# Sample-token projection in float32 on column quarters, and merge gates in a PSUM bank of their own

## The chip, the cores and the metric

One core of one Trainium2 chip runs the whole program. The metric is device time in microseconds of one execution: the median over several executions. PE is the matrix engine (TensorE), PEld its weight loads, DVE, ACT and POOL the vector, scalar and GpSimd engines, SP the queue that issues nearly all DMAs.

## The reference

One layer of a mixer is computed for 1024 prompt tokens and 32 sample tokens ("dec" in the code) that share all weights:

```
h   = rms_norm(x, g_norm) * (1 + scale) + shift            # scale, shift, gate = silu(c) @ w_ada
qa, ka, va, ga, qb, kb, vb, gb, mg = split(h @ w_in)       # 6144 columns, mg is 2048 of them
oa  = diff_attn(rms(qa), rms(ka), va)    # 4 heads, two softmax maps each, block-causal
ob  = band_attn(rms(qb), rms(kb), vb)    # 8 heads, own 64-chunk and the 8 before it
m   = sigmoid(mg_a) * ((oa*silu(ga)) @ w_oa) + sigmoid(mg_b) * ((ob*silu(gb)) @ w_ob)
out = x + gate * (m @ w_out)             # also returned: the keys and values of both branches
```

The sample tokens attend to 128 cached rows besides their own 32. Inputs and outputs are float32.

## The kernel before, in words

Float32 products are made on PE from float32r pieces. `get_w(u, k)` loads a 128x512 weight tile `wr` (a ring of 3 buffers for all weights), ACT rounds it to `wh`, DVE makes the rest `wl = wr - wh`, and a product of two split operands is three matmuls: high by high, high by low, low by high. `wh` and `wl` have 8 buffers each for the projection, and 2 each (`mh`, `ml`) for the merge gates and later weights.

The program has four stages.

1. Start: conditioning (`ada`, float32 matmuls of 32 weight columns, four of them side by side on column quarters of PE, tile `pm`), the RMS norm, and the split input `H[k]`. The 32 sample columns of `H[k]`, high and low side by side, are copied by POOL to `HS[k]` (128x64). Four early row tiles of unit 0 are projected here.
2. Units: eight units, u = 0 to 3 of branch A (512 weight columns) and 4 to 7 of branch B (384, and the gates `pg`). In each, row tiles t = 0 to 7 of 128 prompt tokens and t = 8, the sample tokens, are projected (`proj_items`: eight items k in a row into a bank `pp`), normed (`norm`), transposed (`tr`), scored (`s`), exponentiated, transposed again (`pt`, copied to `pr` by ACT and DVE) and multiplied by the values (`o`); branch A also transposes its result (`zt`). Query and key pieces go through DMAs (`split` to `qs` and `kc`). For t = 8 the projection is 16 float32r matmuls with `HS[k]` as weights (high and low, 64 columns) against `wh` and `wl`; DVE copies and adds the two halves (`dsrc`). After t = 8, `get_w` is called for all of the next unit.
   Of the 48 merge-gate thirds (24 matmuls of 352 columns each into `mg`, a Tanh on ACT, a store `tgd`), `MERGE` puts 24 after chosen row tiles of the units. They take the same two banks `pj` as the projections (the first two take `o` and `pt`) and stand in line with them.
3. Merge rest: the other thirds, while `load_z` brings back the attention results and splits them.
4. Output: `y` (the two branch projections), the merge, and `out`, on PE without a pause.

The order of work is made on the host. A small clock simulation first puts items in program order: attention items that are ready go first, the others ("flat") fill in, not more than `LEAD` row tiles ahead. Then `Plan.flush` schedules every instruction with a cost model: on PE the ready instruction that stands first in program order is taken; on the other engines the one with the longest tail. Instructions are emitted in that order, and each engine runs its own in order. PSUM has eight banks: `pj` 2, `tq` 1, `s` 2, `pt` 2, `o` 1.

Of the kernel before, what the change touches and what calls it, by code (L numbers as in the profile page):

```python
# [35 lines left out]
FIRST = ("o", "pt")  # L36

# [3 lines left out]
MERGE = ((5, 5, 8), (7, 8, 8), (7, 8, 8), (7, 8, 8), (8, 8), (7, 7, 8), (7, 7, 8), (7, 8, 8, 8))  # L41


class Buf:


    def __init__(self, shape, space, make, real=None):
        self.shape, self.space, self.make, self.real = list(shape), space, make, real
        self.writes, self.reads, self.ops, self.dtype = [], [], [], F32
        self.before = self.last = None  # L50
# [69 lines left out]
class Tiles:  # L120


    def __init__(self, pool, space="SB", bufs=1):
        self.pool, self.space, self.bufs, self.tags = pool, space, bufs, {}

    def tile(self, shape, dtype, name, tag=None, bufs=None, padded_shape=None):
# [5 lines left out]
        b.dtype = dtype  # L132
# [19 lines left out]
class Engine:  # L152
# [15 lines left out]
    def cost(self, method, outs, ins, kw):  # L168
# [25 lines left out]
class Plan:  # L194
# [10 lines left out]
    def __init__(self, nc):  # L205
# [4 lines left out]
        self.like, self.urge = None, 0.0  # L210
# [9 lines left out]
    def record(self, eng, cost, f, outs, ins, args, kw):  # L220
# [5 lines left out]
        op.like, op.urge = self.like, self.urge  # L226
# [43 lines left out]
    def flush(self, in_turn=False):  # L270

        self.link()
# [11 lines left out]
        pe = [op for op in self.ops if op.eng == "PE"]  # L284
# [29 lines left out]
        while len(order) < len(self.ops):  # L314
# [32 lines left out]
        for op in sorted(order, key=lambda o: o.start):  # L347
            op.emit()
        for op in self.ops:
            op.preds = op.succs = op.emit = op.acc = None  # L350
        self.ops = []
# [3 lines left out]
def hybrid_mixer_step(ctx: ExitStack, tc: tile.TileContext, xT, cT, two, c_rows, w_as, w_ag, b_ada, g_norm, w_all,  # L355
                      g_rows, g_sub, lam, bias_a, bias_b, ck, cv,
                      y, akp, avp, bkp, bvp, aks, avs, bks, bvs):
    nc = tc.nc
    plan = Plan(nc)
# [16 lines left out]
    BANKS = {"pj": 2, "tq": 1, "s": 2, "pt": 2, "o": 1}  # L376
# [19 lines left out]
    wtiles = {}  # L396

    def get_w(u, k):
# [4 lines left out]
        load(wr, w_all[u, k])  # L403
        split_hi_lo(wh, wl, wr, S, V)
        wtiles[u, k] = (wh, wl)

# [9 lines left out]
    HS = [hp.tile([P, 2, NS], F32R, name=f"HS{k}") for k in range(KT)]  # L416


    with tc.tile_pool(name="start", bufs=1) as spool:
# [106 lines left out]
        def modulate(i, k):  # L526
# [8 lines left out]
            if i:  # L535
                G.tensor_copy(HS[k], H[k][:, :, NP:NT].bitcast(F32))

# [50 lines left out]
    class Item:  # L588
        def __init__(self, emit, dur, lat, bank=None, hold=0.0):
            self.emit, self.dur, self.lat, self.bank, self.hold = emit, dur, lat, bank, hold  # L590

        def ready(self, prev):
            r = prev + self.lat * LATENCY
# [4 lines left out]
        def run(self, prev):  # L598
            clk.now = max(clk.now, self.ready(prev)) + self.dur
            if self.bank:  # L600
                clk.bank_used(self.bank[0], clk.now + self.hold * LATENCY)
            self.emit()
            return clk.now
# [4 lines left out]
    with ExitStack() as uctx:  # L608
# [43 lines left out]
        def proj_items(un, t, st):  # L652
# [4 lines left out]
            def mm(k):  # L657
# [4 lines left out]
                if not dec:  # L662
                    for i, (a, b) in enumerate(((0, wh), (0, wl), (1, wh))):
                        PE.matmul(pp[:, :wcols], lhsT=H[k][:, a, t * P:(t + 1) * P], rhs=b[:, :wcols],
                                  start=(k == 0 and i == 0), stop=(k == 7 and i == 2))
                else:
                    for i, b in enumerate((wh, wl)):
                        PE.matmul(pp[:64, :wcols], lhsT=HS[k].rearrange("p a b -> p (a b)"), rhs=b[:, :wcols],
                                  start=(k == 0 and i == 0), stop=(k == 7 and i == 1))
                if k == 7:  # L670
                    norm()

            def norm():
                src = st["pp"]
                if dec:
                    pp, src = src, up.tile([P, 512], F32, tag="split", name=f"dsrc{u}")
                    V.tensor_copy(src[:n, :wcols], pp[32:64, :wcols])
                    V.tensor_tensor(out=src[:n, :wcols], in0=pp[:n, :wcols], in1=src[:n, :wcols], op=ALU.add)
# [43 lines left out]
            if dec:  # L722
                d *= 2 / 3
# [8 lines left out]
        def attn_items(un, t, st):  # L732
# [176 lines left out]
            for m in range(1 if isA else 2):  # L909
# [4 lines left out]
                for g in range(len(groups)):  # L914
# [4 lines left out]
                                      bk("o") if last else None, 1.0))  # L919
# [4 lines left out]
        def mg_items(i, c, ci, tag):  # L924

            u, d, b = 8 + i, 2 * i + c // 2, c % 2
            o, w = CHN[ci]
            st = {}

            def mm(k):  # L930
                if k == 0:
                    st["p"] = tile_bank(tag, f"mg{d}_{b}_{ci}")
                pg = st["p"]
                wh, wl = wtiles[u, 2 * c + k // 4]
                for j, (a, hb) in enumerate(((wh, 0), (wh, 1), (wl, 0))):
                    PE.matmul(pg[:, :w], lhsT=a[:, (k % 4) * P:(k % 4 + 1) * P], rhs=H[k][:, hb, o:o + w], start=(k == 0 and j == 0), stop=(k == 7 and j == 2))
                if k == 7:
                    tg = up.tile([P, 352], F32, tag="tg", name=f"tg{d}_{b}_{ci}")
                    S.activation(tg[:, :w], pg[:, :w], AF.Tanh, scale=0.5)
                    store(tgd[d, :, b, o:o + w], tg[:, :w])  # L940

            dd = 3 * (w / 2400 + 0.003)
            return [Item(lambda k=k: mm(k), dd, 0.0, bk(tag) if k == 0 else None, 9 * dd + (1.0 if tag == "pj" else 9.0)) for k in range(KT)]


        flat = []
        steps = []
        clk.free = {}
        proj_end = {}
        for t, tag in enumerate(EARLY):  # L950
            proj_end[t] = 1.2 * t
            clk.bank_used(tag, 4.0 + 1.2 * t)
        mgn = [0]

        def mg_chunk(step):
            r = mgn[0]
            if r == 48:
                return
            mgn[0] += 1
            g, ci = r // 3, r % 3  # L960
            flat.extend((step, it, None) for it in mg_items(g // 4, g % 4, ci, FIRST[r] if r < len(FIRST) else "pj"))
            if ci == 2 and g < 15:
                flat[-1] += ([lambda g=g: fm_w(g + 1)],)

        fm_w(0)
        for u in range(8):
            un = UN[u] = Unit(u)
            for t in range(9):
                st = {}
                steps.append((un, t, st))  # L970
                fl = []
                if not un.isA and t in (0, 3, 6):
                    fl += [(it, None) for it in gate_items(un, t // 3)]
                its = proj_items(un, t, st)
                if u == 0 and t < len(EARLY):
                    st["pp"] = early[t]
                    st["norm"]()
                    continue
                fl += [(it, None) for it in its[:-1]] + [(its[-1], len(steps) - 1)]
                flat += [(len(steps) - 1, it, mark) for it, mark in fl]  # L980
                if t == 8:
                    post = [lambda u=u: [get_w(u + 1, k) if u < 7 else fm_w(16 + k) for k in range(8 if u < 7 else 3)]]
                    flat[-1] += (post,)
                for _ in range(MERGE[u].count(t)):
                    mg_chunk(len(steps) - 1)
            if u == 7:
                n_attn = len(flat)
        while mgn[0] < 48:
            mg_chunk(len(steps))

        fi = 0
        active = []
# [252 lines left out]
```

## Time and profile before

| | us |
|---|---|
| median of 3 runs | 1044.6 (1041.18 to 1045.16) |
| the profiled execution, time | 1041.39 |
| the profiled execution, span in the profile | 1039.6 |
| PE busy | 999.7 (96%) |
| DVE, ACT, POOL busy | 660.3, 453.8, 262.7 |

The span runs from the first to the last instruction. All instructions carry line 223, that of the recording helper, so rows are told apart by tile names: `pp<-wh,HS` is a matmul into `pp` that reads `wh` and `HS`. A matmul's shape is given as weight rows * weight columns, then rows x streamed columns. Matmuls overlap: the time that one takes is read from the start of one to the start of the next, not from its duration. The code of a float32 matmul leaves two matmul records (64 in the code of `ada`, 128 in the trace).

### The profile page before, as it was taken

The page shows a single profiled execution, that of the slowest core. Times are in us where ns is not written, and L with a number is a line of the kernel's source. Part 1 is how long each engine was busy: PE and PEld are TensorE (multiplying, and loading weights), DVE is VectorE, ACT ScalarE, POOL GpSimd, SP SyncE. Part 2 cuts the span into 40 slices and gives each one's busy share as a digit, 9 for nine tenths or more (in the row PEclk, how much of TensorE's full clock was granted, in tenths as well). Part 3 has the DMA queues.
Part 4 walks back from the last instruction along what each step waited for, and adds up shares of the span by engine and source line. Part 5 has one row for each costly group of instructions (what it writes and reads, how often), then busy time and mean ns, then how long its engine had stood idle before and what let it go on. Part 6 is the DMA issues. An engine that isn't in the chain of part 4 may idle for free.

```text
span 1039.6 us, 19092 instructions
## 1 busy us (share of the span) xinstructions
PE 999.7 (96%) x6016; PEld 911.6 (88%) x6016; DVE 660.3 (64%) x1936; ACT 453.8 (44%) x1306; POOL 262.7 (25%) x348
## 2 busy tenths in 40 slices
PE   3998989999999999999999999999999999999998
PEld 2666868887887889898999999899989999999998
DVE  4685785784785677588578678767944117975221
ACT  3463564563564455456355445545635212212000
POOL 0254324423433432322221331222200002331000
PEclk9998999999999999999999999999999999999999
DMA  9623433343324225224323322422456327665421
GB/s 328 257 78 84 144 108 79 82 127 98 84 83 143 78 74 168 57 69 125 91 74 112 116 64 77 145 77 70 118 184 196 99 86 227 212 195 174 145 91 49
DMA packets 136803, 126.55 MB, mean 122 GB/s; under 512 B 24064, under 2 KB 113024, under 8 KB 136576
## 3 DMA queue, kind: packets, MB, share of 16 engines
q1 hardware_dynamic: 135696, 124.98, 40.2%
q8 instruction: 49, 0.80, 0.3%
q14 instruction: 50, 0.41, 0.1%
q10 hardware_dynamic: 1008, 0.35, 0.1%
HBM read 75.46 MB, written 23.86 MB: 96 GB/s over the span
## 4 chain that ended last, share of the span: by engine, by line
PE 82%; DVE 5%; DMA 4%; SPq 3%; issue 2%; ACT 2%; POOL 1%; ACTq 0%; DVEq 0%; POOLq 0%
PE pp L223 27%; PE mg L223 16%; PE out L223 9%; PE y L223 9%; PE s L223 6%; PE o L223 5%; PE pg L223 4%; PE pt L223 3%; SPq L223 3%; DMA qs<-split 2%; PE tr L223 1%; DVE T L223 1%; DMA wr<-in_w_all_dram 1%; PE pm L223 1%; DVE x L223 1%
## 5 line engine op out<-in xcount | busy, mean ns | idle before, releaser
L223 PE MATMUL pp<-wh,H 128*128 128x512 f32 (+1 forms) x1024 | 319.1, 377 | 5.1 <-DVE qn L223 2.7
L223 PEld LDWEIGHTS pp<-wh,H 128*128 128x128 f32 x1024 | 187.2, 190 | 28.4 <-DVE H L223 3.2
L223 PE MATMUL pp<-wl,H 128*128 128x512 f32 (+1 forms) x512 | 192.3, 376 | 0.0
L223 PE MATMUL mg<-H,wh 128*128 128x352 f32 x768 | 189.5, 326 | 0.9 <-ACT wh L223 0.9
L223 PEld LDWEIGHTS mg<-H,wh 128*128 128x128 f32 x768 | 133.1, 188 | 3.2 <-ACT wh L223 1.4
L223 ACT ACTIVATE T<-T,nm 128x640 f32<-128x640 f32 (+5 forms) x144 | 101.0, 701 | 76.9 <-DVE nm L223 74.1
L223 DVE TENSOR_TENSOR wl<-wr,wh 128x512 fp32r<-128x512 f32 x128 | 92.9, 733 | 56.0 <-ACT wh L223 55.9
L223 PE MATMUL mg<-H,wl 128*128 128x352 f32 x384 | 124.2, 325 | 0.0
L223 ACT ACTIVATE wh<-wr 128x512 fp32r<-128x512 f32 x128 | 79.6, 629 | 88.9 <-DMA wr<-in_w_all_dram 40.4
L223 PE MATMUL s<-kc,qs 128*128 128x512 f32 (+3 forms) x384 | 100.0, 341 | 7.8 <-DMA qs<-split 7.4
L223 PEld LDWEIGHTS pp<-wl,H 128*128 128x128 f32 x512 | 97.0, 189 | 11.2 <-issue 2.1
L223 POOL TENSOR_TENSOR v<-vraw,v 128x128 fp32r<-128x128 f32 (+1 forms) x72 | 36.0, 502 | 255.5 <-ACT v L223 245.6
L223 DVE CUSTOM_DVE_ANT_0 T<-s,bias 128x512 f32<-128x512 f32 (+2 forms) x144 | 73.8, 512 | 34.0 <-PE s L223 32.4
L223 PE MATMUL y<-Z,wh 128*128 128x352 f32 x384 | 92.4, 323 | 0.0
L223 PE MATMUL out<-MT,wh 128*128 128x352 f32 (+2 forms) x384 | 92.1, 323 | 0.0
L223 DVE TENSOR_TENSOR pr<-pt,pr 128x512 fp32r<-128x512 f32 (+5 forms) x168 | 76.0, 460 | 18.3 <-ACT pr L223 16.4
L223 POOL TENSOR_TENSOR ssq<-ssq,mhalf 128x4 f32<-128x4 f32 (+1 forms) x72 | 75.9, 1054 | 45.5 <-DVE ssq L223 29.8
L223 ACT ACTIVATE pr<-pt 128x512 fp32r<-128x512 f32 (+5 forms) x168 | 65.5, 412 | 49.7 <-PE pt L223 35.2
L223 PEld LDWEIGHTS s<-kc,qs 128*128 128x128 f32 x384 | 66.9, 190 | 17.4 <-issue 9.9
L223 PEld LDWEIGHTS mg<-H,wl 128*128 128x128 f32 x384 | 72.0, 188 | 0.4
L223 POOL TENSOR_TENSOR tgl<-tgl,tgl 128x352 f32<-128x352 f32 x24 | 28.3, 1180 | 174.2 <-DMA tgl<-tgd 107.1
L223 POOL TENSOR_TENSOR qn<-qn,grow 128x256 f32<-128x256 f32 (+1 forms) x72 | 57.4, 799 | 52.1 <-DVE qn L223 29.7
(131 smaller groups left out, 1770.9 us busy)
## 6 DMA issues: line engine op xcount, KB each, us to landing
wr<-in_w_all_dram SPq DMA_DIRECT2D x128, 256.0 KB, 3.1
kc<-split SPq DMA_DIRECT2D x256, 64.0 KB, 2.1
tgd<-tg SPq DMA_DIRECT2D x48, 176.0 KB, 2.5
tgl<-tgd SPq DMA_DIRECT2D x48, 176.0 KB, 3.3
wa<-in_w_as_dram SPq DMA_DIRECT2D x16, 512.0 KB, 8.1
qs<-split SPq DMA_DIRECT2D x256, 32.0 KB, 1.9
zr<-zd SPq DMA_DIRECT2D x24, 176.0 KB, 3.8
wg<-in_w_ag_dram SPq DMA_DIRECT2D x16, 256.0 KB, 3.3
```

The lines of the kernel that those rows point to most:

```text
L223: f(*[r(x) for x in args], **{k: r(v) for k, v in kw.items()})
```

## The change: what it does

- The sample tokens' projection reads `wr`, the unsplit float32 weights. `HS[k]` becomes the float32 sum of the two pieces (128x32); for each k, four (branch B: three) float32 matmuls of 128 columns, one for each 128 weight columns, go to the four column quarters of PE, into 32 partitions each of one bank. ACT copies the bank to SBUF, and later, when t = 7 is normed, copies the quarters side by side.
- For units 1 to 7 these items stand at the head of the unit, after `get_w` of that unit, and not at its end; `get_w` follows t = 7 of the unit before. For unit 0 the eight tiles are loaded once more and the items alternate with those of t = 5.
- Merge thirds get a bank `mg` of their own; `pt` has one bank in place of two. Their matmuls are marked `low`: they are not in PE's program order, and the planner takes one only when no other PE instruction is ready. `MERGE` puts 26 thirds into the units. A load of merge weights is planned to wait until its `wh` buffer is free.
- The clock simulation runs twice; in the second run an item also waits until the buffers that it took in the first are free (`Item.free`).
- The planner's cost of a 32-column float32 matmul goes from 0.0675 to 0.108 us for 256 columns.

```diff
-FIRST = ("o", "pt")
-MERGE = ((5, 5, 8), (7, 8, 8), (7, 8, 8), (7, 8, 8), (8, 8), (7, 7, 8), (7, 7, 8), (7, 8, 8, 8))
+MERGE = 7 * ((0, 0, 1, 0, 1, 0, 1, 0, 0),) + ((0, 0, 1, 0, 1, 0, 1, 1, 2),)
...
-                return 0.0675 * max(n, 64) / 256 if ins[0].shape[-1] == 32 else max(1.69e-3 * n, 0.22)
+                return 0.4225e-3 * max(n, 64) if ins[0].shape[-1] == 32 else max(1.69e-3 * n, 0.22)
...
-        pe = [op for op in self.ops if op.eng == "PE"]
+        pe = [op for op in self.ops if op.eng == "PE" and not op.low]
...
-                heapq.heappush(avail[e], (op.idx if e == "PE" else -op.tail, i, op))
+                heapq.heappush(avail[e], (op.idx + (1e6 if op.low else 0) if e == "PE" else -op.tail, i, op))
...
-    BANKS = {"pj": 2, "tq": 1, "s": 2, "pt": 2, "o": 1}
+    BANKS = {"pj": 2, "tq": 1, "s": 2, "pt": 1, "o": 1, "mg": 1}
...
         load(wr, w_all[u, k])
+        if mg and plan.units:
+            plan.ops[-1].acc.append((wh.view(), False))
         split_hi_lo(wh, wl, wr, S, V)
         wtiles[u, k] = (wh, wl)
+        if u < 8:
+            wraw[u, k] = wr
...
-                G.tensor_copy(HS[k], H[k][:, :, NP:NT].bitcast(F32))
+                G.tensor_tensor(out=HS[k], in0=H[k][:, 0, NP:NT].bitcast(F32), in1=H[k][:, 1, NP:NT].bitcast(F32), op=ALU.add)
...
-                else:
-                    for i, b in enumerate((wh, wl)):
-                        PE.matmul(pp[:64, :wcols], lhsT=HS[k].rearrange("p a b -> p (a b)"), rhs=b[:, :wcols],
-                                  start=(k == 0 and i == 0), stop=(k == 7 and i == 1))
...
+            def mm_dec(k):
+                if u == 0:
+                    wr = wp.tile([P, 512], F32, tag="wr", name=f"wd{k}", bufs=3)
+                    load(wr, w_all[0, k])
+                else:
+                    wr = wraw[u, k]
+                if k == 0:
+                    st["pp"] = tile_bank("pj", f"pp{u}_{t}")
+                for j in range(wcols // P):
+                    PE.matmul(st["pp"][32 * j:32 * j + 32, :P], lhsT=HS[k], rhs=wr[:, j * P:(j + 1) * P], start=(k == 0), stop=(k == 7))
+                if k == 7:
+                    st["raw"] = up.tile([P, P], F32, tag="dsrc", name=f"dsrc{u}")
+                    S.activation(st["raw"][:wcols // 4], st["pp"][:wcols // 4, :P], AF.Copy)
...
                 if dec:
-                    pp, src = src, up.tile([P, 512], F32, tag="split", name=f"dsrc{u}")
-                    V.tensor_copy(src[:n, :wcols], pp[32:64, :wcols])
-                    V.tensor_tensor(out=src[:n, :wcols], in0=pp[:n, :wcols], in1=src[:n, :wcols], op=ALU.add)
+                    src = up.tile([P, 512], F32, tag="split", name=f"src{u}")
+                    for j in range(wcols // P):
+                        S.activation(src[:n, j * P:(j + 1) * P], st["raw"][32 * j:32 * j + 32], AF.Copy)
...
+        def mg_third(r):
+            g, ci = r // 3, r % 3
+            d, b = g // 2, g % 2
             o, w = CHN[ci]
+            plan.low = True
+            pg = tile_bank("mg", f"mg{d}_{b}_{ci}")
+            for k in range(KT):
+                wh, wl = wtiles[8 + g // 4, 2 * (g % 4) + k // 4]
                 for j, (a, hb) in enumerate(((wh, 0), (wh, 1), (wl, 0))):
                     PE.matmul(pg[:, :w], lhsT=a[:, (k % 4) * P:(k % 4 + 1) * P], rhs=H[k][:, hb, o:o + w], start=(k == 0 and j == 0), stop=(k == 7 and j == 2))
+            tg = up.tile([P, 352], F32, tag="tg", name=f"tg{d}_{b}_{ci}")
+            S.activation(tg[:, :w], pg[:, :w], AF.Tanh, scale=0.5)
+            store(tgd[d, :, b, o:o + w], tg[:, :w])
+            plan.low = False
             if ci == 2 and g < 15:
+                fm_w(g + 1)
...
+                        if t == 7:
+                            fl[-1] = (its[7], now, [dec[u]["norm"]])
+                    flat += [(now, it, mark, post or []) for it, mark, post in fl]
+                    if t == 7:
+                        flat[-1][3].extend(lambda k=k, u=u: get_w(u + 1, k) if u < 7 else fm_w(16 + k) for k in range(8 if u < 7 else 3))
+                    if t == 8 and u < 7:
+                        dec.append({})
+                        flat += [(now, it, None, []) for it in proj_items(UN.setdefault(u + 1, Unit(u + 1)), 8, dec[-1])]
+                    flat[-1][3].extend([merge] * MERGE[u][t])
...
+        back = plan.mark()
+        kept = dict(wtiles), dict(wraw)
+        lay_out()
+        back()
...
-        return tile_bank(("pj", "s", "pt")[banks[0] % 3], name)
+        return tile_bank(("pj", "s", "mg", "pj", "s", "pt")[banks[0] % 6], name)
```

## Rows read from the trace of the kernel before

**Rows 1.** The page: engines, chain of work that ended last, by engine.

```profile
PE 999.7 (96%) x6016; PEld 911.6 (88%) x6016; DVE 660.3 (64%) x1936; ACT 453.8 (44%) x1306; POOL 262.7 (25%) x348
...
PE 82%; DVE 5%; DMA 4%; SPq 3%; issue 2%; ACT 2%; POOL 1%; ACTq 0%; DVEq 0%; POOLq 0%
```

**Rows 2.** Busy by stretch: eight units, merge rest, output (PE, PEld, DVE, ACT, POOL; clock, DMA).

```profile
60.00:108.00 48.00, 41.13 (x184) 32.57 (x183) 32.45 (x104) 23.49 (x78) 25.30 (x37) 0.89 0.35 94
108.00:204.00 96.00, 92.30 (x507) 76.28 (x506) 69.25 (x227) 54.48 (x175) 36.37 (x54) 1.00 0.37 103
204.00:297.00 93.00, 90.44 (x499) 75.68 (x498) 62.45 (x192) 47.74 (x150) 33.38 (x48) 1.00 0.35 98
297.00:381.00 84.00, 83.62 (x455) 69.75 (x454) 56.76 (x184) 43.83 (x142) 33.71 (x48) 1.00 0.36 102
381.00:466.00 85.00, 83.40 (x528) 78.81 (x527) 61.02 (x187) 44.44 (x131) 22.89 (x32) 1.00 0.35 97
466.00:562.00 96.00, 94.73 (x612) 90.03 (x611) 74.98 (x241) 49.95 (x153) 25.55 (x33) 1.00 0.32 88
562.00:649.00 87.00, 86.37 (x553) 82.08 (x552) 66.82 (x214) 44.81 (x136) 22.31 (x29) 1.00 0.36 99
649.00:757.00 108.00, 104.97 (x676) 99.06 (x675) 83.88 (x264) 58.95 (x174) 25.73 (x34) 1.00 0.38 109
757.00:850.00 93.00, 92.43 (x575) 91.87 (x574) 24.52 (x52) 30.48 (x69) 0.00 (x0) 1.00 0.42 133
850.00:1040.00 190.00, 186.39 (x1161) 186.18 (x1159) 95.86 (x198) 30.22 (x55) 28.33 (x24) 1.00 0.50 157
```

**Rows 3.** PE's timeline in unit 0, where it sits idle; start, duration, idle before.

```profile
91.00 0.40 PE L223 MATMUL o<-v,pr 128*128 128x256 f32 x2
93.15 0.59 PE L223 MATMUL s<-kc,qs 128*128 128x384 f32 x2 [1.75 <-DMA qs<-split]
...
98.08 1.19 PE L223 MATMUL s<-kc,qs 128*128 128x512 f32 x2 [0.62 <-DMA qs<-split]
```

**Rows 4.** Busy time by stretch, same columns, where the clock is slow.

```profile
96.47:106.71 10.24, 8.71 (x23) 5.85 (x23) 5.64 (x18) 3.43 (x10) 1.44 (x2) 0.50 0.32 82
```

**Rows 5.** PE's timeline: sample-token matmuls of 512 columns, then of 384.

```profile
109.90 0.39 PE L223 MATMUL pp<-wl,HS 128*64 128x512 f32 x1
110.13 0.40 PE L223 MATMUL pp<-wh,HS 128*64 128x512 f32 x1
...
466.55 0.34 PE L223 MATMUL pp<-wl,HS 128*64 128x384 f32 x1
466.72 0.33 PE L223 MATMUL pp<-wh,HS 128*64 128x384 f32 x1
```

**Rows 6.** PE's timeline: float32 matmuls on column quarters among full ones.

```profile
25.66 1.07 PE L223 MATMUL pm<-wa,c 128*32 128x256 f32 x16
26.66 0.50 PE L223 MATMUL pp<-wh,H 128*128 128x512 f32 x1
...
28.60 0.64 PE L223 MATMUL pm<-wa,c 128*32 128x256 f32 x8
29.17 0.50 PE L223 MATMUL pp<-wh,H 128*128 128x512 f32 x1
29.51 0.39 PE L223 MATMUL pp<-wl,H 128*128 128x512 f32 x1
29.73 0.63 PE L223 MATMUL pp<-wh,H 128*128 128x512 f32 x2
30.29 0.64 PE L223 MATMUL pm<-wa,c 128*32 128x256 f32 x8
```

**Rows 7.** PE's timeline: float32r matmuls of 32 weight columns among full ones.

```profile
231.44 0.31 PE L223 MATMUL s<-kd,qs 128*32 128x160 f32 x2
231.59 0.66 PE L223 MATMUL pp<-wh,H 128*128 128x512 f32 x2
232.09 0.39 PE L223 MATMUL pp<-wl,H 128*128 128x512 f32 x1
```

**Rows 8.** Groups of instructions, shapes apart, 60 to 757 us: busy, mean ns.

```profile
L223 DVE TENSOR_TENSOR wl<-wr,wh 128x512 fp32r<-128x512 f32 x79 | 56.6, 727 | 6.3 <-ACT wh L223 6.1
L223 ACT ACTIVATE wh<-wr 128x512 fp32r<-128x512 f32 x80 | 49.8, 631 | 18.5 <-DMA wr<-in_w_all_dram 16.7 <-PE mg L223 1.0
L223 DVE TENSOR_TENSOR pr<-pt,pr 128x512 fp32r<-128x512 f32 x64 | 43.5, 685 | 8.5 <-ACT pr L223 8.0
L223 ACT ACTIVATE pr<-pt 128x512 fp32r<-128x512 f32 x64 | 37.5, 593 | 27.1 <-PE pt L223 16.1 <-PE o L223 10.6
L223 DVE COPY dsrc<-pp 32x512 f32<-32x512 f32 x4 | 2.7, 682 | 0.1
L223 ACT ACTIVATE vraw<-dsrc 32x128 f32<-32x128 f32 x8 | 2.3, 293 | 0.0
```

**Rows 9.** DMA issues by line: count, KB each, median us to landing.

```profile
wr<-in_w_all_dram SPq DMA_DIRECT2D x128, 256.0 KB, 3.1
qs<-split SPq DMA_DIRECT2D x256, 32.0 KB, 1.9
```

**Rows 10.** Instructions that touch `wr`: duration ns min/median/max, first and last start.

```profile
L223 SPq DMA_DIRECT2D wr<-in_w_all_dram x128: 327/371/1507, 8.3 to 980.4; - x128
```

More of the change, by code (lines that the diff above doesn't have):

```diff
@@ L209, in __init__ @@
         self.rows = {"DVE": None, "ACT": None}
-        self.like, self.urge = None, 0.0
+        self.like, self.urge, self.low, self.units = None, 0.0, False, True
         self.V, self.S, self.G, self.PE = (Engine(self, n, e) for n, e in (
@@ L270, in flush, with mark, back, lay_out @@
     def flush(self, in_turn=False):
+        for op in self.lay_out(in_turn):
+            op.emit()
+        for op in self.ops:
+            op.preds = op.succs = op.emit = op.acc = None
+        self.ops = []
+    def mark(self):
+        bufs = [(b, list(b.writes), list(b.reads), list(b.ops)) for b in Buf.made]
+        rings = [(r, {t: list(q) for t, q in r.tags.items()}) for r in Tiles.made]
+        free, ring, rows = dict(self.free), self.ring, dict(self.rows)
+        def back():
+            del Buf.made[len(bufs):]
+            for b, w, r, o in bufs:
+                b.writes, b.reads, b.ops = list(w), list(r), list(o)
+            for r, tags in rings:
+                r.tags = {t: list(q) for t, q in tags.items()}
+            self.free, self.ring, self.rows, self.ops = dict(free), ring, dict(rows), []
+        return back
+    def lay_out(self, in_turn=False):
         self.link()
@@ L346, in flush @@
                     heapq.heappush(pend[q.eng], (q.ready, q.idx, q))
[L347 to L351, printed above, removed]
+        return sorted(order, key=lambda o: o.start)
 @with_exitstack
@@ L415, in hybrid_mixer_step @@
     H = [hp.tile([P, 2, NT], F32R, name=f"H{k}") for k in range(KT)]
-    HS = [hp.tile([P, 2, NS], F32R, name=f"HS{k}") for k in range(KT)]
+    HS = [hp.tile([P, NS], F32, name=f"HS{k}") for k in range(KT)]
     with tc.tile_pool(name="start", bufs=1) as spool:
@@ L589, in __init__, with free @@
         def __init__(self, emit, dur, lat, bank=None, hold=0.0):
-            self.emit, self.dur, self.lat, self.bank, self.hold = emit, dur, lat, bank, hold
+            self.emit, self.dur, self.lat, self.bank, self.hold = emit, dur, lat * LATENCY, bank, hold * LATENCY
+            self.key = None
+        def free(self):
+            count = {}
+            for place in takes.get(self.key, ()):
+                pool, tag, n = place
+                ring, i = pool.tags.get(tag, ()), count.get((pool, tag), 0)
+                count[pool, tag] = i + 1
+                j = len(ring) + i - n
+                if 0 <= j < len(ring):
+                    for key in users.get(ring[j].name, set()) - done:
+                        if not (isinstance(key, tuple) and isinstance(self.key, tuple) and key[0] == self.key[0]):
+                            return False
+            return True
         def ready(self, prev):
-            r = prev + self.lat * LATENCY
+            r = prev + self.lat
             if self.bank:
@@ L600, in run @@
             if self.bank:
-                clk.bank_used(self.bank[0], clk.now + self.hold * LATENCY)
+                clk.bank_used(self.bank[0], clk.now + self.hold)
+            n, m = len(plan.ops), len(Buf.made)
             self.emit()
+            done.add(self.key)
+            takes[self.key] = [b.place for b in Buf.made[m:]]
+            for op in plan.ops[n:]:
+                for v, _ in op.acc:
+                    users.setdefault(v.buf.name, set()).add(self.key)
             return clk.now
@@ L965, in hybrid_mixer_step @@
[L965 to L977, printed above, removed]
-                    continue
[L979 to L987, printed above, removed]
@@ L1056, in load_z @@
         Z.append(z)
-    for r in range(48 - (len(flat) - fi) // KT, 48):
+    for r in range(mgn[0], 48):
         g, ci = r // 3, r % 3
```

185 lines of the change are left out of this document (104 added, 81 removed).

## Prediction

> **What bounds the kernel now.** I read the page first: PE is busy for 96% of the span and holds 82% of the chain that ended last; no other engine is over 64% [rows 1]. So time can come only from less PE work, from PE's pauses, or from its clock. Next I cut the span by unit [rows 2]: each line's length less PE's busy time is its idle time there. The eight units (60 to 757 us) idle for 6.9, 3.7, 2.6, 0.4, 1.6, 1.3, 0.6 and 3.0 us, 20.0 together; the merge rest loses 0.6, and the output's 3.6 lie at its very end. The early units hold the pauses: in unit 0 PE starts two matmuls at 91.00 and nothing until 93.15, for a `qs` transfer, and four such waits follow each other [rows 3]. Then the granted clock is 0.50, the 1.2 GHz level, from 96.47 to 106.71 [rows 4], right behind these pauses; 10.24 us at half speed cost up to 5.1 us. Gate work can therefore win at most 20.0 + 5.1 = 25 us, and where it stands costs nothing elsewhere, since the merge rest and the output run on PE almost without pause either way.
>
> The profiled execution took 1041.4 us (span 1039.6); the median of the runs is 1044.6, 3.2 more. I sum on 1041.4 and add 3.2.
>
> **Sample tokens: what is removed.** 8 units x 16 matmuls with 64 weight columns. From start to start one takes 0.23 us at 512 columns (109.90 to 110.13) and 0.17 at 384 (466.55 to 466.72) [rows 5]. 64 x 0.23 + 64 x 0.17 = 25.6 us of PE.
>
> **What is added.** 64 rounds (8 units x 8 k) of four or three float32 matmuls on column quarters. The nearest rows are those of `pm`, the same form with 256 columns [rows 6]; eight records there are four matmuls in the code, one round. One round lasts 0.57 us until the next matmul starts (28.60 to 29.17), two lasted 1.00 (25.66 to 26.66): a further round costs 0.43, so 0.14 is paid once. The matmul behind takes 0.34 (29.17 to 29.51) and not 0.23: 0.11 more. The two ahead take 0.56 (29.73 to 30.29) and not 0.46: 0.10 more. So a group of rounds costs 0.43 for each round and 0.35 for the way in and out. With 128 columns I take half, 0.215 a round: 64 x 0.215 = 13.8 us. If the column count did not matter it would be 27.5; the quarters start together and the streaming sets the pace, so I stay near the half.
>
> How many groups? At least 8, one a unit (2.8 us); at most 64, each round by itself (22.4 us). The rounds need `wr`, of which there are three buffers. Three tiles can lie there early; the other five come only as buffers are freed, and a load lands 3.1 us after its issue [rows 9], after which ACT needs 0.63 and DVE 0.73 [rows 8]. PE is never without other work for so long, so it goes back to full-width matmuls between them. I count eight groups in unit 0, where the items alternate with others, and four to five in each other unit: 39 groups, 13.7 us. Sum 27.5 against 25.6: **+1.9 us**, with ends of -9.0 (8 groups: 16.6) and +10.6 (64 groups: 36.2).
>
> The Trainium skill speaks against the change here: "TensorEngine Tiling (Array Packing)", section "Key Properties", says that changing the tiling mode drains the engine. By `pm` [rows 6] that holds, and the sum is the +1.9 above. By the float32r matmuls with 32 weight columns it does not show: two of 160 columns take 0.15 (231.44 to 231.59), and the two full ones behind them 0.50 (231.59 to 232.09) [rows 7], hardly over 0.46; by these the switches would be free and the sum -11.8. The new matmuls are float32 and use all quarters, as `pm` does, so I stay with `pm`.
>
> **The rest of that edit.** Eight loads of 256 KB more in unit 0, where the DMA engines are busy for 0.35 of the time [rows 2]: hidden, but SP issues them past the `qs` transfers that PE waits for [rows 3]; 0 to +3 us (eight issues of 0.37 [rows 10]); I take 0. DVE loses two instructions of 0.68 a unit, ACT gains one copy from PSUM and three or four of about 0.29 each [rows 8], some 11 us in all on an engine that is busy for 44%; the result is wanted only by the last row tile of the unit, so I take 0. If that cover were gone it would be 1.4 us a unit. The sum for `HS` on POOL replaces a copy of the same kind: 0.
>
> **Merge gates.** The 24 matmuls of each third stay; only their place moves. Before, a third stood in line with the projections and held one of their two banks. After it, single matmuls of it can stand in PE's pauses. What it can win is the 20.0 + 5.1 us above. It will not win all: the order is fixed on the host, so a matmul stands where the cost model sees a pause, while PE stops where a transfer or an engine is later than the model thought; and a third needs its weights and its Tanh first. The long pauses of units 0 to 2 (13.2 us) come from the latency of a chain that any model shows, the others from small misses. I take three fifths, **-12 us**, and half of the slow clock, **-2.6**. Lower end: nothing; upper: -25.
>
> **One `pt` bank.** A group of four transposes is copied out by ACT (0.59) and DVE (0.69) [rows 8], 1.28 us in which the next group cannot start. Where a row tile has a second group (16 times in A, 32 in B) that wait is new. Other row tiles and gate matmuls are there to fill it. I take **+2**; at worst 48 x 1.28 = 61, at best 0.
>
> **Weights earlier.** `get_w` of the next unit no longer waits for 16 matmuls of t = 8, which frees `wh` and `wl` earlier; PE has no pause for weights in the rows to win back, so 0. But a `wr` buffer is now also held until PE has done its round, and merge weights stand in the same ring: see the third rival.
>
> **Sum.** 1041.4 + 1.9 - 12 - 2.6 + 2 = 1030.7 for an execution like the profiled one; with 3.2, **1034 us**. Its own range is 1025 to 1039 (nearly all of the pauses won, or few).
>
> **Rivals.**
>
> 1. *Rounds run together and pauses vanish.* Three early tiles and late ones that pile up give two groups a unit: 13.8 + 16 x 0.35 = 19.4, -6.2. Of the pauses 17 us go, and the slow clock (-5.1) since PE does not pause ahead of it; the bank costs 0. 1041.4 - 6.2 - 17 - 5.1 + 3.2 = 1016. For it: the two long early waits are easy to fill, and 11.5 us of gate work with one set of weights are at hand. Against it: the three-buffer ring. Chance 0.18.
> 2. *The quarters do not pay.* Every round stands alone, +10.6, and the gates win as forecast: 1041.4 + 10.6 - 12 - 2.6 + 2 + 3.2 = 1043. For it: nothing makes the planner keep rounds together, its cost has no price for the way in and out. In this case the first half of the change does not do what it says. Chance 0.15.
> 3. *The ring of `wr` becomes the bound at the unit boundaries (slower).* A tile's buffer is released after load, split and now PE's round; gate weights in the same ring wait for gates that PE takes last. One turn of the ring is 3.1 + 0.63 + 0.73 = 4.5 us [rows 8, 9]. If one more turn at each of 7 boundaries finds PE without work, it is +31: 1065. It makes the kernel slower by more than 0.5% from (5.2 + 10.6)/7 = 2.3 us a boundary on. For it: eight tiles need three turns. Against it: PE never pauses for `wh` in the units now, and low gates are there as filler. Chance 0.14.
> 4. *The single `pt` bank binds.* If half of the 61 us are not filled: +31 in place of +2, 1063. Against it: ACT and DVE are idle for more than a third of the time. Chance 0.06.
>
> **How the numbers follow.** The forecast has 0.47. About 0.5%, 5 us, is what a measurement of this kernel can tell from no change: the runs of before spread by 4 us. Faster by more than that (under 1039.4) are the forecast and rival 1: 0.65. Within it is rival 2: 0.15. Slower are rivals 3 and 4: 0.20. The range of 8 in 10 reaches into rival 1 and over rival 2 into the smaller sizes of 3 and 4: 1012 to 1058.
>
> **What would show it.** In the profile after: PE idle time in the units near 8 us; unit 0 without waits of over 1 us for `qs`; a shorter stretch, or none, at clock 0.50; 256 records of sample matmuls into `pp` with 32 weight columns in A and 192 in B, each round some 0.22 to the next round or 0.5 to 0.6 if alone, in about 39 groups. It would be wrong if the groups were near 8 or 64, if `pp` or `pg` waited for ACT `wh` or DVE `wl` at the boundaries, if `pt` waited for DVE `pr` by tens of microseconds, or if PE's pauses stayed near 20 us.

## The result, and the profile after

The changed kernel takes 1072.8 us (median of 4 runs, 1066.8 to 1073.6), the kernel before 1042.9 (4 runs, 1040.5 to 1045.2): a ratio of 1.0274 [1.0227, 1.0321]. It is slower by 2.7%; the forecast was 1034 us, faster. The profiled execution took 1073.6, its span 1071.7.

The page after, engines and the chain that ended last (all instructions now carry line 227):

```profile
PE 1018.8 (95%) x6336; PEld 910.1 (85%) x6336; DVE 655.3 (61%) x1920; ACT 465.8 (43%) x1342; POOL 258.0 (24%) x348
...
PE 75%; DMA 9%; SPq 6%; DVE 5%; ACT 3%; issue 1%; POOL 0%; ACTq 0%; DVEq 0%; POOLq 0%
```

Against [rows 1] PE is busy for 19 us longer, and PE's share of the chain fell from 82% to 75% while DMA and SP's queue rose from 7% to 15%. So there are two losses: more PE work, and PE waiting for transfers. What PE waited for (total, times, longest):

```profile
PE pp L227 <- DMA wr<-in_w_all_dram: 10.8, 16, 1.1
PE pp L227 <- DMA wd<-in_w_all_dram: 3.8, 3, 2.8
PE mg L227 <- ACT tg L227: 3.1, 4, 1.2
PE s L227 <- DMA qs<-split: 2.8, 4, 1.2
PE pt L227 <- DVE pr L227: 2.6, 5, 1.0
```

The waits for `qs` of [rows 3] fell, in the whole program from 7.6 us to 2.8. In their place the rounds of the sample tokens wait for their weights, `wr` (`wd` in unit 0). PE's timeline at the end of unit 5:

```profile
579.18 0.42 PE L227 MATMUL pp<-wr,HS 128*32 128x128 f32 x6 [0.84 <-DMA wr<-in_w_all_dram]
...
585.06 0.42 PE L227 MATMUL pp<-wr,HS 128*32 128x128 f32 x6
585.41 0.62 PE L227 MATMUL pg<-H,wh 128*128 128x384 f32 x2
...
590.23 0.42 PE L227 MATMUL pp<-wr,HS 128*32 128x128 f32 x6 [0.66 <-DMA wr<-in_w_all_dram]
...
592.59 0.42 PE L227 MATMUL pp<-wr,HS 128*32 128x128 f32 x6 [0.93 <-DMA wr<-in_w_all_dram]
```

Each of these rounds stands alone between full-width matmuls; the second takes 0.35 us to the next start (585.06 to 585.41).

**The unit boundary.** I call so the stretch from the last prompt projection of a unit to the first of the next. The windows of the boundaries, before:

```profile
550.20:577.50 27.30, 26.82 (x180) 25.48 (x179) 23.00 (x63) 16.62 (x43) 7.29 (x9) 1.00 0.45 126
...
sum 175.80, PE 173.14 PEld 158.72 DVE 150.59 ACT 113.13 POOL 53.98; mean PE 24.73 PEld 22.67 DVE 21.51 ACT 16.16 POOL 7.71
```

and after:

```profile
562.20:596.60 34.40, 30.60 (x217) 25.03 (x216) 25.08 (x69) 19.31 (x49) 5.62 (x8) 1.00 0.49 137
...
sum 173.50, PE 156.51 PEld 128.04 DVE 131.19 ACT 104.97 POOL 41.43; mean PE 22.36 PEld 18.29 DVE 18.74 ACT 15.00 POOL 5.92
```

The seven boundaries are as long as before, but PE's idle time in them rose from 2.7 us (175.8 - 173.1) to 17.0. What stands in the one at 562 to 597 after: first the gate matmuls, then what reads or writes `wr` (ten splits on DVE and on ACT), the same stretch both times:

```profile
562.20:596.60 34.40, 15.12 (x66) 10.64 (x66) 1.34 (x3) 1.00 0.49 137
...
562.20:596.60 34.40, 3.35 (x48) 1.21 (x48) 6.92 (x10) 6.31 (x10) 1.00 0.49 137
```

66 of a unit's 72 gate matmuls are done only here, where PE takes them last, and no tile of the next unit has been split by then: the ten splits here are the unit's eight and two of gate weights. The instructions on `pp` and `wr` say the same (duration; first and last start):

```profile
L227 PE MATMUL pp<-wh,H x32: 333/338/423, 548.9 to 562.2; 128*128 128x384 f32 x32
...
L227 SPq DMA_DIRECT2D wr<-in_w_all_dram x10: 367/523/593, 572.3 to 589.7; - x10
L227 ACT ACTIVATE wh<-wr x7: 630/631/632, 575.2 to 586.5; 128x512 fp32r<-128x512 f32 x7
```

The first load is issued 10 us behind the last projection. What stood ahead of it, the chain of work that ended last tells for the same stretch (start, duration, what):

```profile
570.20 0.61 DVE pr L227
570.95 0.62 SPq L227
571.62 0.62 SPq L227
572.28 0.59 SPq L227
...
575.23 0.59 SPq L227
575.87 3.27 DMA wr<-in_w_all_dram
...
588.76 3.78 DMA wr<-in_w_all_dram
```

It runs through SP's queue. From 563.9 us on, twelve issues of `qs` and `kc` pieces, some 0.6 us each, stand there ahead of the first load, and three more ahead of the one at 575.23, which the round at 579.18 waits for. Then come two transfers of tiles, the second of which lands when the boundary is nearly over.

Late loads and gates at the boundary are not new, though. Before, in the same boundary, 72 gate matmuls stood there, and the first load was issued 13.8 us behind the last projection (550.2 to 564.0), behind pieces of the same kind; all eight tiles are split in it, and PE idles for 0.5 us:

```profile
550.20:577.50 27.30, 14.12 (x72) 11.67 (x72) 1.37 (x3) 1.00 0.45 126
...
L223 SPq DMA_DIRECT2D wr<-in_w_all_dram x8: 332/370/593, 564.0 to 577.5; - x8
```

What differs is what stands beside them in PE's order: then the gates and 16 sample matmuls on tiles that were already there, now rounds that need the tiles in flight.

**The sum.** I added up the gaps between the starts of PE's matmuls from 60 us to the output, by what they are (a matmul's own streaming time, the way in and out of the quarters, a slow clock, and the rest as waits). Waits counted so are larger than the idle times of the windows, where a matmul's modelled end covers part of a gap. Before 791.0 us, after 822.7; the 31.7 more are +9.5 for the sample matmuls (24.4 to 33.9), +28.5 for waits at boundaries (7.6 to 36.1, 25.0 at the seven shown and 11.2 behind the last unit, before 4.6 and 2.9), -11.3 for waits within units (28.3 to 17.0), +2.6 for slow clock and +2.4 for other small gaps.

### The profile page after: what moved, and what is told of

The parts are those of the page before. It is cut to its first block, busy times and chain, and to the rows that moved or that the text cites. A ratio compares the mean times of both kernels' runs of the same rounds, so it can differ in the third digit from the quotient of the medians.

```text
span 1071.7 us, 19704 instructions
## 1 busy us (share of the span) xinstructions
PE 1018.8 (95%) x6336; PEld 910.1 (85%) x6336; DVE 655.3 (61%) x1920; ACT 465.8 (43%) x1342; POOL 258.0 (24%) x348
## 4 chain that ended last, share of the span: by engine, by line
PE 75%; DMA 9%; SPq 6%; DVE 5%; ACT 3%; issue 1%; POOL 0%; ACTq 0%; DVEq 0%; POOLq 0%
PE pp L227 27%; PE mg L227 12%; PE out L227 9%; PE y L227 9%; SPq L227 6%; DMA wr<-in_w_all_dram 6%; PE o L227 5%; PE s L227 4%; PE pg L227 4%; PE pt L227 3%; DMA qs<-split 1%; PE tr L227 1%; PE pm L227 1%; DVE T L227 1%; DVE x L227 1%
## 5 line engine op out<-in xcount | busy, mean ns | idle before, releaser
L227 PE MATMUL pp<-wh,H 128*128 128x512 f32 (+1 forms) x1024 | 326.6, 380 | 0.0
L227 PE MATMUL mg<-H,wh 128*128 128x352 f32 x768 | 198.0, 332 | 5.5 <-ACT tg L227 3.1
L227 PE MATMUL mg<-H,wl 128*128 128x352 f32 x384 | 126.7, 331 | 1.8 <-DVE wl L227 1.1
L227 ACT ACTIVATE pr<-pt 128x512 fp32r<-128x512 f32 (+5 forms) x168 | 67.9, 412 | 70.0 <-PE pt L227 67.6
L227 POOL TENSOR_TENSOR ssq<-ssq,mhalf 128x4 f32<-128x4 f32 (+1 forms) x72 | 74.3, 1034 | 41.5 <-DVE ssq L227 38.7
L227 PE MATMUL pt<-ident,T 128*128 128x128 f32 (+2 forms) x408 | 71.1, 272 | 2.7 <-DVE pr L227 2.6
L227 POOL TENSOR_TENSOR tgl<-tgl,tgl 128x352 f32<-128x352 f32 x24 | 28.3, 1178 | 178.3 <-DVE tgl L227 171.0
```

Source lines behind the costliest of these rows:

```text
L227: f(*[r(x) for x in args], **{k: r(v) for k, v in kw.items()})
```

## The experiments

Theory: the rounds, now at the head of a unit, wait for weight tiles that come too late, since a ring of three buffers is held up by gate weights and gates taken last. Rival A: the price of the quarters alone (62 lone groups). Rival B: the boundary lacks ready work, now that 16 sample matmuls that needed nothing are gone from the unit's end. Ratios are to the kernel before.

**The halves.** `e1` keeps the gate half and puts back the old sample tokens; `e2` keeps the new sample tokens, with the gates in line in the banks `pj`, two `pt` banks, and no planned wait of a gate weight's load for its `wh` buffer.

```diff
# e1
+ for i, b in enumerate(wtiles[u, k]):
+     PE.matmul(st["pp"][:64, :wcols], lhsT=HS[k]..., rhs=b[:, :wcols], ...)     # at t = 8, as before
# e2
+MERGE = ((5, 5, 8), (6, 8, 8), (6, 8, 8), (6, 8, 8), (8, 8), (6, 6, 8), (6, 6, 8), (7, 8, 8, 8, 8, 8))
+    BANKS = {"pj": 2, "tq": 1, "s": 2, "pt": 2, "o": 1}
```

> The changed kernel with its sample-token half undone: float32r matmuls with wh and wl at the end of the unit as before; gates keep their own bank, low, and pt has one. Theory A (the loss is the sample tokens: lone rounds 9.5 us, PE's waits for wr and wd 16.7): some 26 us under the changed kernel, 1040 to 1050, near the kernel before. Theory B (the loss is the gate half: one bank for the gates, one for pt, low gates that hold the weight ring): only the 9.5 come back, 1060 to 1066.

> The changed kernel with its gate half undone: 26 gate thirds as items in program order in the two pj banks, two pt banks; the sample tokens stay in float32 on quarters at the head of the unit. Theory A: as slow as the changed kernel, 1065 to 1075, with waits of PE for wr above 10 us. Theory B: the gate waits go, 1050 to 1056, waits for wr under 5 us because no low gates hold the ring.

`e1` took 1048.9 us, 1.0046 [1.0022, 1.007]; `e2` 1068.2, 1.0218 [1.0179, 1.0258]. Most of the loss needs the new sample tokens, and low gates aren't needed for a loss of this kind: in `e2`, where some of the thirds stand at the boundary in order, PE waits 13.0 us for `wr` and idles for 15.3 us in its seven boundaries (149.6 - 134.3):

```profile
sum 149.60, PE 134.31 PEld 111.89 DVE 107.46 ACT 84.08 POOL 56.05; mean PE 19.19 PEld 15.98 DVE 15.35 ACT 12.01 POOL 8.01
...
L227 SPq DMA_DIRECT2D wr<-in_w_all_dram x6: 332/371/372, 579.6 to 586.2; - x6
```

There the loads aren't late: at the sixth boundary (578.8 to 598.4) one is issued 0.8 us behind the last projection, at all seven one within 2.5 us. Part of `e2`'s time is the clock, 0.979 to 0.989 in the mean of its four runs, where the kernel before has 0.993 to 0.997.

**The quarters.** `e3` runs the rounds in groups of 3, 3 and 2 tiles; `e7` leaves the items at the head of the unit, but as 64-column float32r matmuls on `wh` and `wl`.

```diff
# e3
+GROUP = ((0, 1, 2), (3, 4, 5), (6, 7))
+def mm_dec(g):
+    for k in GROUP[g]:
+        for j in range(wcols // P): PE.matmul(st["pp"][32 * j:32 * j + 32, :P], lhsT=HS[k], rhs=wraw[u, k]...)
# e7
+    for i, b in enumerate(wtiles[u, k]):
+        PE.matmul(st["pp"][:64, :wcols], lhsT=HS[k]..., rhs=b[:, :wcols], ...)
```

> The changed kernel with its 64 rounds planned in groups of 3, 3 and 2 (the first matmul of a group also counts as reading the other tiles). Theory A: some 24 groups in place of about 60, 36 x 0.35 = 12.6 us less; waits for wr about as before or less: 1052 to 1062. Theory B: the way in and out is not what costs: 1068 to 1075.

> The changed kernel with the sample tokens kept at the head of the unit, but as float32r matmuls of 64 weight columns on wh and wl; the raw buffers no longer wait for PE and no quarters are used. Theory A1 (place: matmuls at the head wait for weights that are still in flight): the waits stay, now for ACT wh and DVE wl, and only the 9.5 us of the lone rounds come back: 1058 to 1066. Theory A2 (ring: the raw buffers held until PE's round hold up the weights): rounds and waits both go, 1044 to 1050.

`e3`: 1.0206 [1.0168, 1.0244]; 25 groups in place of 62, the sample matmuls fall from 33.9 to 26.4 us, the boundaries' waits rise from 36.1 to 38.3. `e7`: 1.0176 [1.015, 1.0201], without any quarters. So rival A is worth some 1.0 of the 2.7% (1.0274 to 1.0176; `e7` also drops the eight extra loads of unit 0). What is left over `e1` (1.0046), 1.3%, comes with the place at the head of the unit, though projections of any kind wait for `wh` and `wl` for only 1.9 us there; by the intervals the two shares can't be told apart.

**The late tiles.** `e5` lets the planner count a round's weights as landed 2 us later. `e8` loads the weights a second time in every unit and does the rounds among the projections of t = 5; `e9` is that in threes, `e10` the same on the kernel before.

```diff
# e5
+                    plan.ops[-1].late = 2.0
# e8
+                wr = wp.tile([P, 512], F32, tag="wr", name=f"wd{u}_{k}", bufs=3)
+                load(wr, w_all[u, k])
...
+                            if t == 5: fl.append((its_dec[k], None, None))
# e9, e10: e8 with GROUP of e3
```

> The changed kernel, where the planner counts a round's weights as landed 2 us later; nothing else. Theory A in the form that PE runs into transfers which land later than planned: waits for wr and wd fall from 14.6 us to under 5, time 1060 to 1065. If the waits come from the ring itself (buffers free too late), the plan only moves them: 1068 to 1080.

> The changed kernel, where every unit loads its eight weight tiles once more for the sample tokens and the float32 rounds alternate with t = 5, as unit 0 does it; 14.7 MB more are read. Theories A1 and A2 both: PE's waits for wr fall from 14 us to a few, the rounds stay alone (about 60 groups, +9.5): 1053 to 1060. If the waits have another cause (the gates): 1068 to 1076.

> The same with the rounds in groups of 3, 3 and 2: 24 groups, so 12 us less than the run with lone rounds: 1042 to 1050. What is left over the kernel before is then the gate half, 4 to 5 us by the run with the sample tokens undone.

> The kernel before with only the sample tokens changed: float32 on quarters, weights loaded once more, groups of 3, 3 and 2 among t = 5; gates and banks as before. Float32 rounds cost 13.8 + 24 x 0.35 = 22.2 us against 25.6, so -3.4 if nothing else moves: 1038 to 1046. If taking a projection bank during t = 5 and the freed place at the unit's end cost PE its filler: 1050 to 1056.

`e5`: 1.0266 [1.0234, 1.0298]. Its waits show why that gains nothing:

```profile
PE pg L229 <- ACT wh L229: 5.9, 7, 2.2
PE s L229 <- DMA qs<-split: 5.2, 6, 1.5
...
PE pp L229 <- DMA wd<-in_w_all_dram: 2.1, 1, 2.1
```

The waits for `wr` are off the list, and the next work at the boundary, `pg`, waits for the split of the same tiles. `e8` 1.0322 [1.0293, 1.0351], `e9` 1.0324 [1.0295, 1.0353], `e10` 1.0433 [1.0407, 1.0459]: the boundaries' waits fall to 13.8, 13.8 and 14.4 us, but those within units rise from 17.0 to 41.5, 54.4 and 53.3. A second load doesn't take the wait away; in `e10` it is spread over `qs` (10.4), `pt` for DVE (8.4) and `pp` for DVE (6.9). `e10` also has a mean granted clock of 0.983, some 37 us at the 1.2 GHz level against 10 before. Why the units wait so much more I did not separate.

**Where the gate weights stand in the ring.** `e12` (on `e1`), `e13` (on the change) and `e14` (on `e3`) put the thirds so that the load of the next gate weights comes behind the unit's tiles.

```diff
+MERGE = ((0, 0, 0, 0, 1, 0, 1, 0, 1),) + 6 * ((0, 0, 1, 0, 1, 0, 0, 0, 1),) + ((0, 0, 1, 0, 1, 0, 1, 1, 1),)
```

> The run with the sample tokens undone, and the gate thirds so placed (t = 2, 5 and 8; 4, 6 and 8 in unit 0) that the load of the next gate weights stands behind the next unit's eight tiles in the ring of raw buffers, not ahead of them. Ring theory (low gates hold the raw ring through the unit, so the unit's first load starts 13 to 17 us after its predecessor's last projection): loads start early again, waits at the boundaries fall by 5 to 8 us: 1037 to 1044. If the ring is not what holds: 1046 to 1051.

> The changed kernel with that same placing of the thirds. Ring theory: units 2 to 6 get their first three tiles early as units 0 and 1 do now, the boundaries shrink from 33 to about 22 us, and 10 to 15 us of the 37.5 us of waits there go: 1057 to 1063. Filler theory: tiles come earlier, but PE still lacks ready work and the lone rounds stay: 1066 to 1073.

> The same with the rounds planned in groups of 3, 3 and 2. Both theories: 6 to 9 us under the run with lone rounds, as between the changed kernel and its run in threes.

1.0051 [1.0027, 1.0074], 1.023 [1.0178, 1.0281] and 1.023 [1.0191, 1.0269]. The sixth boundary of `e13`, gates and `wr`, is that of the change:

```profile
556.80:591.20 34.40, 15.11 (x66) 10.65 (x66) 1.35 (x3) 1.00 0.48 137
...
556.80:591.20 34.40, 3.35 (x48) 1.21 (x48) 6.92 (x10) 6.31 (x10) 1.00 0.48 137
```

The order of loads in the program, as I had put it, is not the cause: with either placing PE leaves the low thirds to the boundary, and the loads are issued as late. Whether the ring would matter if they came early, these runs can't show.

**Ready work.** `e11` is the kernel before without 14 of the 16 sample matmuls of a unit (only k = 0 is multiplied, so the sample tokens' projection is left out but for an eighth). `f1` adds to the change 16 float32r matmuls at t = 8 whose result nobody uses, with the next unit's loads behind them; `f2` and `f3` give the change and `e1` two thirds more in each unit but the last.

```diff
# e11
-                else:
+                elif k == 0:
# f1
+    PE.matmul(st["fill"][:64, :wcols], lhsT=H[k][:, 0, 0:64], rhs=b[:, :wcols], ...)
# f2, f3
+MERGE = 7 * ((0, 0, 1, 0, 1, 0, 1, 1, 1),) + ((0, 0, 1, 0, 1, 0, 1, 1, 2),)
```

> The kernel before without 14 of every 16 sample-token matmuls (only k = 0 is left, so that the sample tokens' projection is wrong): 22.4 us less PE work at the unit's end, nothing else edited. If PE is short of ready work there (filler theory: the old matmuls fill time in which PE would wait for weights and softmax), the time falls by no more than half of that: 1031 to 1040. If PE's work simply adds up: by 20 to 23, 1019 to 1023.

> The changed kernel plus filler: at the place of t = 8 the 16 float32r matmuls of the kernel before stand again (64 weight columns on wh and wl), their result unused; the next unit's loads follow them as before. 24.4 us more PE work in all. Filler theory (PE waits at the boundaries because ready work is missing there): most of it hides, the boundary waits of 36 us fall by 12 or more: 1074 to 1084. Additive: 1092 to 1099.

> The changed kernel with two more gate thirds in each unit (after t = 7 and 8), taken from the merge rest; the PE work in all is the same. Filler theory: low gates fill the boundaries, waits of 53 us fall to under 43 and the time to 1056 to 1064. If PE does not lack work but stands behind one waiting matmul while others are ready, gates cannot help: 1069 to 1076.

> The run with the sample tokens undone, with the same two more thirds in each unit. Filler theory: its 44 us of waits fall to under 36: 1038 to 1044, at or under the kernel before. Otherwise 1047 to 1052.

`e11`: 1.0019 [1.0001, 1.0038]. 21 us of PE work are gone (24.4 to 3.1) and nothing is gained: waits rise by 20.3 us (35.8 to 56.1) and the clock costs 8 more by the gaps. `f1`: 1.045 [1.0418, 1.0483]; 24.4 us of ready work more cost 18, and the boundaries' waits go only from 36.1 to 33.2. `f2`: 1.0277 [1.0239, 1.0314], no different from the change. So more work at the boundary, of either kind, does not cure it, and nothing supports rival B as the main cause; a filler that leaves the loads where they were was not tried. `f3`: 1.022 [1.0196, 1.0245], where `e1` had 1.0046: with more low thirds the old sample tokens lose as well, and their boundaries' waits go from 17.6 to 38.4.

**The low mark.** `f5` is `e1` with no gate marked low, in the same places. `g1` (on `e1`) and `g2` (on the change) have the gates of units 0 to 6 in program order, in their own bank, at t = 2, 4 and 6; only the eight thirds of unit 7 (six in the change; two come from the merge rest), moved to its end, are low, and those of the merge rest.

```diff
# f5
-            plan.low = True
+            plan.low = False
# g1, g2
-MERGE = 7 * ((0, 0, 1, 0, 1, 0, 1, 0, 0),) + ((0, 0, 1, 0, 1, 0, 1, 1, 2),)
+MERGE = 7 * ((0, 0, 1, 0, 1, 0, 1, 0, 0),) + ((0, 0, 0, 0, 0, 0, 0, 2, 6),)
-            plan.low = True
+            plan.low = r >= 20
```

> The run with the sample tokens undone, and the gates no longer low: they keep their own bank but stand in PE's program order where they are called (after t = 2, 4 and 6). If taking gates only in pauses is what helps, this is slower than 1049 by 5 us or more, since no gates are left for the boundaries; if low gates are what costs the 4 us over the kernel before, 1042 to 1047.

> The run with the sample tokens undone; gates have their own bank and stand in PE's program order in units 0 to 6, and only the eight thirds of unit 7's end are low. By the run without low gates, boundaries 0 to 6 then wait for 3 us and not 12; the 23 us of its last boundary get gates again and fall to 6 or less: 1034 to 1042, under the kernel before. If low gates are not what PE stands behind: 1046 to 1052.

> The changed kernel with the same gates. If PE's boundary waits come from low gates that stand in PE's queue ahead of ready work: the 24 us of waits at boundaries 0 to 6 fall to 10 or less, time 1052 to 1062. If they come from the sample tokens at the head of the unit, whose weights are in flight: waits there stay above 18, time 1066 to 1074.

`f5`: 1.0097 [1.0077, 1.0117]; 2.6 us of waits are left at the seven boundaries together (PE idles there for 2.4 us, in `e1` for 8.1), but 16.9 stand behind the last unit, where no gate is left to fill in. In that part of `f5` the granted clock is also 0.50 for 23.9 us, with PE busy for 17.1 of them, where `e1` has 1.00 from its last projection to 855 us. By these 17.1 it costs up to 8.6 us, an estimate, and is part of why `f5` is no faster:

```profile
754.80:778.70 23.90, 17.11 (x63) 13.73 (x64) 12.76 (x48) 7.69 (x26) 0.00 (x0) 0.50 0.11 35
```

`g1` has gates in order and filler at the end: 1039.6 us (12 runs), 0.9949 [0.9927, 0.9972], the fastest of all. `g2`: 1044.9, 1.0017 [0.9999, 1.0035]. Its boundaries, then gates and `wr` in the sixth:

```profile
554.70:570.10 15.40, 15.40 (x130) 12.73 (x129) 11.90 (x34) 9.28 (x26) 4.76 (x6) 1.00 0.48 136
...
sum 96.00, PE 94.25 PEld 75.44 DVE 77.61 ACT 62.64 POOL 35.95; mean PE 13.46 PEld 10.78 DVE 11.09 ACT 8.95 POOL 5.14
...
554.70:570.10 15.40, 3.12 (x17) 2.69 (x17) 0.00 (x0) 1.00 0.48 136
...
554.70:570.10 15.40, 2.95 (x48) 1.34 (x48) 3.47 (x5) 3.13 (x5) 1.00 0.48 136
```

The boundaries shrink from 173.5 to 96.0 us and PE idles in them for 1.8 and not 17.0; 17 gate matmuls stand there, not 66, and three tiles of the next unit are split beforehand. PE's waits in the whole program:

```profile
PE s L227 <- DMA qs<-split: 1.9, 5, 0.6
...
PE pp L227 <- DMA wr<-in_w_all_dram: 1.5, 2, 1.1
```

The four kernels side by side, ratio to before and PE's idle time at the seven boundaries (before: 2.7 us):

| | gates low in every unit | gates in order, low only at the end |
|---|---|---|
| old sample tokens | `e1` 1.0046, 8.1 us | `g1` 0.9949, 3.7 us |
| new sample tokens | the change 1.0274, 17.0 us | `g2` 1.0017, 1.8 us |

With the low gates the new sample tokens cost 2.3%, with gates in order 0.7%, some 7 us: by the gaps the sample matmuls of `g2` take 6.9 us more than those of `g1` (31.3 and 24.4, in 53 groups). Low gates, together with the other place of unit 7's thirds, cost 1.0% with the old and 2.6% with the new sample tokens; taking the mark away alone, in `f5`, did not make `e1` faster, since it also took the filler from the end.

## Why the prediction was wrong

**What bounds.** PE's pauses in the units could be won as read: waits within units fell by 11.3 us, where I had taken 12 for the gates. The step that failed is that where gate work stands "costs nothing elsewhere", and with it the 0 under "Weights earlier" for the sample tokens' new place. In their place the runs showed +28.5 us of waits, 20.4 of them at the seven boundaries: there the rounds stand in PE's order and wait for tiles in flight, among gates that the unit left over. Neither a boundary full of gates nor the new sample tokens did that alone: with gates in order beside the old sample tokens PE idled there for 2.7 us (before), with the new ones and most gates done within the unit for 1.8 (`g2`). With low gates it idled for 8.1 beside the old ones (`e1`) and for 17.0 beside the new.

**Rival 3** had the place and held a chance of 0.14. I gave it 4.5 us a boundary and 1065 us; by the gaps, waits at the seven boundaries rose by those 20.4 (25.0 - 4.6), 2.9 each, over the 2.3 from which it decides, and by 8.3 more behind the last unit. What I set against it, low gates as filler, is part of it: without the mark, in the same places, PE idles for 2.4 us at the boundaries of `f5`, with it for 8.1 (`e1`), and with more low thirds for 18.0 (`f3`). Its mechanism is shown in part. That low thirds which are not done within the unit bring a loss is shown by `f3`, `f5`, `g1` and `g2`. Their number at the boundary is not enough, since the kernel before has as many there, and late loads are neither enough (before) nor needed (`e2`). Why a round and a gate left over hurt each other stays open: whether it is the third's `wh`, which a load of gate weights is planned to wait for, the ring, or the planner's order was not separated. `e12` to `e14` changed the placing, and neither the loads nor the time followed; a load of gate weights without that planned wait was tried only in `e2`, together with other banks and places. `g1` and `g2` also move unit 7's thirds, so the low mark and that move are apart only by `f5`, and only for the old sample tokens.

**What is removed.** The 25.6 us are 24.4 by the gaps. But to count them as time was wrong: `e11` leaves out 21 of them from the kernel before and gains nothing. They needed no transfer, and stood in the stretch in which the next unit's tiles arrive (boundaries of 175.8 us before, 2.7 idle); without them PE waits there or in the units. In `f1` this could not be turned round: the same work, put back beside the new rounds and ahead of the loads, isn't hidden.

**What is added.** The prices held: a lone round takes 0.35 to the next start in the timeline above, and about 0.09 more on each side, 0.53, where I had 0.215 + 0.35 = 0.57. By this price of going in and out the trace agrees with the Trainium skill's rule that changing the tiling mode drains the engine ("TensorEngine Tiling (Array Packing)", "Key Properties"), which I followed against [rows 7]. The number of groups was mis-sized: 62, not 39, so that the term measured +9.5 and not +1.9. That is rival 2's size. I had argued that rounds which wait are separated by other work, and then counted too few.

**The rest.** Slow clock: not -2.6 but +2.6; it came in three stretches, 6.83, 3.40 and 3.40 us:

```profile
65.87:72.70 6.83, 6.05 (x21) 4.54 (x22) 6.83 (x18) 4.87 (x17) 4.49 (x6) 0.50 0.04 12
106.80:110.20 3.40, 3.40 (x12) 2.83 (x11) 1.63 (x7) 1.57 (x6) 1.27 (x2) 0.50 0.35 85
779.30:782.70 3.40, 3.40 (x15) 3.38 (x14) 2.38 (x8) 1.36 (x5) 0.00 (x0) 0.50 0.47 152
```

They are 13.6 us against the 10.2 of [rows 4], the longest one now earlier. The `pt` bank: 2.6 us of waits for DVE `pr`, the +2 that I took; rival 4 is out. Eight loads more in unit 0: PE waits 3.8 us for `wd`, where I had taken 0 and up to 3. Rival 1 needed few groups and no new wait, and had neither.

The 31.7 us of the gaps account for nearly all of the difference between the two profiled executions (1041.4 + 31.7 = 1073.1, measured 1073.6).

## What to carry to other kernels

Work that is taken only when nothing else is ready fills pauses, but it also holds its buffers until then, and what of it is left over meets the next stage: mark work as filler only where nothing later needs what it holds (in `g1` the end of the last unit), and do the rest in order, early enough that the next loads can start. Before work is removed or moved from a stretch, ask what arrives during that stretch: PE work that needs no transfer may be what covers it, and work that needs one must not stand in order at the moment of its arrival. A price for each switch of shape has to be multiplied by a number of switches counted under the worst supply of data, since transfers that come one by one make every piece stand alone.

## What the runs showed of the hardware

Less PE work went with a lower clock: `e11`, with 21 us of matmuls left out, had a mean granted clock of 0.985, about 31 us of its 1045 at the 1.2 GHz level, where before had 10:

```profile
core 0: 1045.0 us, clock 0.985
```

Its ten runs have 0.985 to 0.990, those of the kernel before beside them 0.990 to 0.997. Its waits within units had risen to 40.0 us from 28.3.

A round of float32 quarter matmuls of 128 columns is short beside the way in and out. In `g2` three rounds run in one group (18 records, three matmuls a round) and take 0.79 us to the next start (556.23 to 557.02):

```profile
556.23 0.86 PE L227 MATMUL pp<-wr,HS 128*32 128x128 f32 x18
557.02 0.59 PE L227 MATMUL mg<-H,wh 128*128 128x352 f32 x2
```

A lone round takes 0.35, so a further one costs 0.22, half of the 0.43 with 256 columns in [rows 6]; of the 0.53 us of a lone round the rest, some 0.31, is the way in and out.
